# A Hymba trunk layer on one core: shorter TensorE warming, a gated and finer first load, one pair's Gram order, one row factor by square root

## The chip, the core and the metric

The kernel runs on one core of one Trainium2 chip. The metric is the device time of one execution in microseconds; lower is better. The kernel before was timed three times: 999.9, 1000.18 and 1000.47 us, median 1000.18 us.

The engines of the core have short names in the profile: PE is TensorE (matmuls), PEld its weight loads, DVE VectorE, ACT ScalarE, POOL GpSimd, SP SyncE, which here only issues transfers. L714 is line 714 of the kernel.

## The reference

One layer over 16 learned meta tokens and 512 real tokens (L = 528), width D = 2048. Cut to what matters:

```
hn = rmsnorm(h, norm_in_g)                  # 528 x 2048
P  = hn @ w_in                              # 2048 x 8320: r,k,v,g (1024 each), lora (128), B,C,h,gc (1024 each)
r,k,v,g,wl,al = shift(P[:, :4224])          # each token mixed with the one before
decay = exp(-exp(-softplus(-(w0 + tanh(wl) @ w_lora_up)) - 0.5))
a     = sigmoid(a0 + al @ a_lora_up)
kk    = normalised per head (k * k_k) ;  k = k * (1 + (a - 1) * k_a)
S_t   = S_{t-1} diag(decay_t) - (S_{t-1} kk_t)(kk_t a_t)^T + v_t k_t^T ;  y_t = S_t r_t   # 16 heads of 64
y_a   = (groupnorm(y) + bonus(r, k, v)) * silu(g)
y_b   = B * causal_conv3(C * h) * silu(gc)
h     = h + concat(y_a, y_b) @ w_out
out   = rmsnorm(h, norm_f_g)[16:]           # 512 x 2048, float32
```

## The kernel before

All large products are done in three parts to keep fp32 accuracy on a faster matmul type: each operand is split into a high part (a rounding cast, usually on ACT) and a low part (the difference, on DVE or POOL), and hi·xh, lo·xh and hi·xl are accumulated in PSUM.

**The input projection and its filler.** The normalised input is kept transposed as 16 k-tiles of 128 rows: `xh` and `xl`, made by `split_x` (L205, ACT at L207 and DVE at L208). `w_in` has 65 column tiles of 128. A load of 512 KB (`wr`, L142) brings half a tile's weights; `prefetch` and `split_w` (L132 to L144) split it into two pieces of 128x512 by an ACT cast (L134) and a DVE or POOL subtract (L135). The matmuls of one column tile run over the token ranges 0..264 and 264..528 (`FULL`), or others for tiles that leave out meta tokens, and over 16 k-tiles. The Python generator `mains()` (L483) gives all these matmuls one by one in the order of `plan`: first four column tiles (lora, k0, r0, B0) side by side, k-tile by k-tile, so that they can start as x arrives; then k, r, v, g of each head pair and C, h, B, gc. `use` reads a finished column tile.

**The order on TensorE is written out by hand.** Work that depends on other engines is issued in small steps, and between two steps `fill(ns)` (L551) takes as many matmuls from `mains()` as the given number of nanoseconds. The table `FW` (L43 to L46) holds these numbers. `until("k", i)` instead drains the generator to a named tile, so after it the order no longer depends on earlier fills. So TensorE always has matmuls of the projection to run while ACT, DVE and POOL prepare the next step.

**A head pair.** `prepare(i)` (L627, i = 0..7) computes decay and a by the low-rank products (tiles `tz`, `ta`; L571, L572, then ACT L578, POOL L639, a scan on DVE at L641 that gives `cc`), then builds the Gram matrices of nine 64-token chunks and two heads (L682) in PSUM tiles of four, four and one chunk: `za` (chunks 0 to 3), `zc` (4 to 7), `ze` (8). DVE multiplies each with a mask into `gt` (L692, six instructions). `ze` takes its two banks from the pool "main" of four banks, which the projection's column tiles (`ps_k`, `ps_r`, `ps_C` and the like) use too; `zc` takes "misc" and "ser", one bank each. After a fill come the norms (`zn`, L713, L714) and `zb` (L716), which use the banks of `zc` and `za` again. Further on, `invert` solves the triangular systems of two pairs, and `recur` (L938) runs the recurrence over the chunks; its matmuls at L957 read `ct`, which a DMA loads from the scratch `opd` in DRAM. Ahead of it stands `fill(FW["begin"])`.

**The start.** A memset of `cold` (128x512, fp32) on DVE feeds two warming matmuls into `pwarm` (L187). SP then issues four loads from `front`, an array in which the first weights and x lie in the order of use: `in_bt` (the norm gains, one weight piece of lora, x0), `in_r` (three pieces for k0, r0, B0), `in_bk` (four pieces for k-tile 1, x1) and `in_gt` (pieces for k-tiles 2 and 3, x2 and x3). Loads of weights and of x4 to x11 follow on SP. `split_piece` (L224) splits a weight piece on ACT and DVE.

**The end.** The output projection adds `mix @ w_out` to the residual; each of four blocks of 128 rows (`row` t = 0..3) gets its sum of squares (`squares`, ACT with an accumulator, L1229), and `row_scale` (L1396) makes the factor 1/sqrt: an add of the partial sums and a power -0.5 on POOL (`rsqrt`, L97). Row 1 is last: its two half blocks of 256 columns (`ends`) are added at L1453, its gain is multiplied in by `gain`, and `finish_last` scales and stores it.

Of the kernel before, what the change touches and what calls it, by code (L numbers as in the profile page):

```python
# [18 lines left out]
P = 128  # L19
DM = 2048  # L20
KT = DM // P
SEQ = 512
META = 16
L = SEQ + META
CH = 64
NCH = SEQ // CH + 1
# [18 lines left out]
    tr=3200, lev=3000, cp=4200, out=1500, begin=20300, p=2900, u=2900, s=4800, last=3700, mix=2600,  # L45
# [32 lines left out]
def hymba_kernel(ctx: ExitStack, tc: tile.TileContext, xt, xtok, front, w_in, w_out, pv, lup, cst, msk, gf, out):  # L78
# [104 lines left out]
    cold = tp.tile([P, 512], F32, tag="tm", name="cold", bufs=3)  # L183
    nc.vector.memset(cold, 0.0)
    pwarm = pi.tile([P, 512], F32, tag="ser", name="pwarm")
    for _ in range(2):
        nc.tensor.matmul(pwarm, cold[:, 0:P], cold, start=True, stop=True)  # L187
# [42 lines left out]

    for n in range(4):
        quarters[2 * n] = slot_of(2 * n)
    F0, F1, F2 = KT + P + L, 4 * P + L, 8 * P + 2 * L
    fr = [view("bt", F0), view("r0", 3 * P), view("bk", F1), view("gt0", F2)]
    o = 0
    for t in fr:
        nc.sync.dma_start(t, front[:, o : o + t.shape[1]])
        o += t.shape[1]
    ng = fr[0]
    raw[0], raw[1] = fr[0][:, KT + P : F0], fr[2][:, 4 * P : F1]  # L240
    for k in range(2):
        raw[2 + k] = fr[3][:, 8 * P + k * L : 8 * P + (k + 1) * L]
# [3 lines left out]
    nc.scalar.activation(warm, warm, AF.Tanh)  # L246
# [4 lines left out]
    with tc.manual_schedule(engines={mybir.EngineType.DVE, mybir.EngineType.Activation}):  # L251
        split_piece(0, 0, fr[0][:, KT : KT + P])
        split_x(0, slice(0, L // 2))
        split_x(0, slice(L // 2, L))
        for n in (1, 2, 3):
            split_piece(n, 0, fr[1][:, (n - 1) * P : n * P])
        split_x(1)
        for n in range(4):
            split_piece(n, P, fr[2][:, n * P : (n + 1) * P])
        for kt in (2, 3):  # L260
            split_x(kt)
            if kt == 2:
# [12 lines left out]
        head = split_x(8)  # L275
# [37 lines left out]
    HALF = SEQ // 2  # L313
# [313 lines left out]
    def prepare(i):  # L627
# [768 lines left out]
    def row_scale(t, n, eng=nc.gpsimd):  # L1396
        f = fv[:, t]
        w, v, r = f[:, 0:1], f[:, 1:2], f[:, 2:3]
        eng.tensor_scalar(out=v, in0=ssq[:, t, n : n + 1], scalar1=w, scalar2=None, op0=ALU.add)
        rsqrt(r, v)  # L1400
        scales[t] = r
# [25 lines left out]
    with tc.manual_schedule(engines={mybir.EngineType.DVE, mybir.EngineType.Activation, mybir.EngineType.Pool}):  # L1427
# [3 lines left out]
        for t in (2, 3):  # L1431
            row_part(t, 3)
            row_scale(t, 3)
        row_part(0, 3)
# [25 lines left out]
        row_scale(1, 4, nc.vector)  # L1460
        gain(1, 2, nc.vector, slice(256, 512))
        finish_last(1)


def _layout(i):
# [35 lines left out]
    front += [t[:, 1] for t in first] + [xt[:, 1]] + [t[:, 2:4].reshape(P, 256) for t in first] + [xt[:, 2], xt[:, 3]]  # L1501
# [24 lines left out]
```

## Time and profile before

| quantity | value |
|---|---|
| median of three runs | 1000.18 us |
| the profiled execution, its own time | 999.89 us |
| its span in the trace (first to last instruction) | 998.0 us |
| granted TensorE clock, mean | 0.998 |
| HBM traffic over the span | 139.28 MB read, 38.71 MB written, 178 GB/s |
| weight splits on ACT (L134) | 252 casts, 153.4 us busy |
| weight splits on POOL and DVE (L135) | 119 and 133 subtracts, 168.2 and 98.3 us busy |

The profile page gives each engine's busy time, the chain of work that ended last, and groups of instructions. In rows of the timeline the columns are the start in us from the span's start, the time in us to the end of the row's last instruction, engine, line, operation, output and inputs with shapes, how many instructions stand in the row (x4), and in brackets how long the engine had waited just before and what released it. In rows of waits the three numbers are the total in us, how often, and the longest. In the windows the columns are the stretch, its length, and the busy time of PE, PEld, DVE, ACT, POOL (with the count of instructions), the granted clock, the DMA engines' share and GB/s. Records of neighbouring matmuls overlap, since matmuls are pipelined; the distance of two starts is what one costs.

### The profile page before, as it was taken

The numbers are of one execution on the slowest core, as the hardware profiler recorded it, in microseconds if no ns is written. First come the engines' busy times: TensorE is split into PE (matmuls) and PEld (weight loads), VectorE is DVE, ScalarE is ACT, GpSimd is POOL, SyncE is SP. The second block draws the span as 40 slices with busy tenths as digits, with TensorE's granted clock in tenths as the row PEclk, the third lists the DMA queues.
The fourth block names the chain that finished last, engine by engine and source line by source line (L and its number), as shares of the span: only waits on it lengthen the run. The fifth ranks groups of instructions, "written<-read, shape, count | busy, mean of one in ns | idle before, by whom it ended". The sixth has DMA issues, their size and how long they took to land.

```text
span 998.0 us, 22792 instructions
## 1 busy us (share of the span) xinstructions
PE 986.7 (99%) x9211; PEld 910.8 (91%) x9211; DVE 689.2 (69%) x1314; ACT 412.2 (41%) x770; POOL 271.6 (27%) x286
## 2 busy tenths in 40 slices
PE   9999999999999999999999999999999999999996
PEld 8999999999998999998999998989889898888885
DVE  7777975487774579735579735246555598999895
ACT  7554432343523535232534232233332326645553
POOL 0122423133422324222324222223242423011001
PEclk9999999999999999999999999999999999999999
DMA  9527585437584365854265954978783698798634
GB/s 324 160 79 184 122 224 144 119 106 179 128 215 140 95 180 130 230 145 111 85 180 120 232 143 114 347 266 283 223 266 96 169 266 232 230 293 224 144 99 168
DMA packets 184985, 179.48 MB, mean 180 GB/s; under 512 B 112176, under 2 KB 141616, under 8 KB 184368
## 3 DMA queue, kind: packets, MB, share of 16 engines
q1 hardware_dynamic: 182288, 169.12, 58.2%
q0 software_dynamic: 2304, 8.39, 4.8%
q8 instruction: 72, 1.18, 0.5%
q10 hardware_dynamic: 288, 0.52, 0.1%
q14 instruction: 33, 0.27, 0.1%
HBM read 139.28 MB, written 38.71 MB: 178 GB/s over the span
## 4 chain that ended last, share of the span: by engine, by line
PE 95%; DMA 2%; DVE 1%; issue 1%; POOL 0%; ACT 0%; DVEq 0%; SPq 0%; POOLq 0%
PE ps_g L328 9%; PE ps_r L328 9%; PE ps_h L328 9%; PE ps_gc L328 9%; PE ps_B L328 9%; PE ps_v L328 9%; PE ps_C L328 8%; PE ps_k L328 8%; PE M L1242 8%; PE P L1242 4%; PE Q L1242 2%; PE g L682 2%; DMA ct<-opd 1%; PE ps_lora L328 1%; PE rz L957 1%; PE zs L1004 1%
## 5 line engine op out<-in xcount | busy, mean ns | idle before, releaser
L134 ACT CAST w<-wr 128x512 fp32r<-128x512 f32 x252 | 153.4, 619 | 280.0 <-PE ps_h L328 47.4
L135 POOL TENSOR_TENSOR w<-wr,w 128x512 fp32r<-128x512 f32 x119 | 168.2, 1415 | 365.2 <-ACT w L134 326.7
L135 DVE TENSOR_TENSOR w<-wr,w 128x512 fp32r<-128x512 f32 x133 | 98.3, 743 | 98.6 <-ACT w L134 97.6
L328 PE MATMUL ps_r<-xh,w 128*128 128x256 f32 (+1 forms) x512 | 95.2, 282 | 1.0 <-DVE gt L692 1.0
L328 PE MATMUL ps_k<-xh,w 128*128 128x256 f32 (+1 forms) x512 | 95.4, 284 | 0.0
L328 PE MATMUL ps_v<-xh,w 128*128 128x272 f32 (+1 forms) x512 | 95.4, 284 | 0.0
L328 PE MATMUL ps_h<-xh,w 128*128 128x258 f32 (+1 forms) x512 | 93.1, 281 | 0.0
L328 PE MATMUL ps_C<-xh,w 128*128 128x258 f32 (+1 forms) x512 | 92.5, 281 | 0.0
L328 PE MATMUL ps_g<-xh,w 128*128 128x258 f32 (+1 forms) x512 | 91.7, 280 | 0.0
L328 PE MATMUL ps_B<-xh,w 128*128 128x512 f32 x256 | 83.1, 394 | 0.0
L328 PEld LDWEIGHTS ps_r<-xh,w 128*128 128x128 f32 x512 | 80.2, 189 | 1.6 <-DVE gt L692 1.2
L328 PE MATMUL ps_gc<-xh,w 128*128 128x512 f32 x256 | 81.6, 393 | 0.0
L328 PEld LDWEIGHTS ps_k<-xh,w 128*128 128x128 f32 x512 | 80.3, 189 | 0.3
L328 PEld LDWEIGHTS ps_v<-xh,w 128*128 128x128 f32 x512 | 80.1, 189 | 0.3
L328 PEld LDWEIGHTS ps_h<-xh,w 128*128 128x128 f32 x512 | 79.5, 189 | 0.3
L328 PEld LDWEIGHTS ps_C<-xh,w 128*128 128x128 f32 x512 | 79.2, 189 | 0.6
L328 PEld LDWEIGHTS ps_g<-xh,w 128*128 128x128 f32 x512 | 79.2, 189 | 0.2
L328 PE MATMUL ps_k<-xl,w 128*128 128x256 f32 (+1 forms) x256 | 73.0, 285 | 0.0
L328 PE MATMUL ps_v<-xl,w 128*128 128x256 f32 (+1 forms) x256 | 72.5, 283 | 0.0
L328 PE MATMUL ps_h<-xl,w 128*128 128x256 f32 (+1 forms) x256 | 72.5, 283 | 0.0
L328 PE MATMUL ps_g<-xl,w 128*128 128x256 f32 (+1 forms) x256 | 72.4, 283 | 0.0
L328 PE MATMUL ps_r<-xl,w 128*128 128x256 f32 (+1 forms) x256 | 72.1, 282 | 0.0
(312 smaller groups left out, 2204.3 us busy)
## 6 DMA issues: line engine op xcount, KB each, us to landing
wr<-in_w_in_dram SPq DMA_DIRECT2D x126, 512.0 KB
ct<-opd SPq DMA_DIRECT2D x56, 320.0 KB
wo<-in_w_out_dram SPq DMA_DIRECT2D x21, 512.0 KB
opd<-gt SPq DMA_DIRECT2D x16, 576.0 KB
x<-in_w_out_dram POOLq DMA_DIRECT2D x16, 512.0 KB, 5.7
opd<-ar SPq DMA_DIRECT2D x8, 576.0 KB
opd<-bt SPq DMA_DIRECT2D x64, 64.0 KB
ct<-opd SPq DMA_DIRECT2D x16, 256.0 KB
```

The lines of the kernel that those rows point to most:

```text
L134: nc.scalar.copy(hi, rq)
L135: low[q] = eng.tensor_tensor(out=lo, in0=rq, in1=hi.bitcast(F32), op=ALU.subtract).ins
L328: nc.tensor.matmul(ps[r], ww[:, w], xx[:, kt, a:b], start=(kt == 0 and n == 0), stop=(kt == KT - 1 and n == 2))
L682: nc.tensor.matmul(z[h][:, c - c0], bk[hs, c, h : h + 2, :].rearrange("p a s -> p (a s)"), ar[hs, c].rearrange("p a s -> p (a s)"), start= ...
L957: nc.tensor.matmul(z[e][ho if e else hs, 0, k], ct[e][hs, k, o : o + CH], uv(e, k, hs, h) if part else st[hs, 4 * e + k], start=(part == 0 ...
L1004: nc.tensor.matmul(zs[hs, j], bb[:, h], uv(e, k, everything, h), start=True, stop=True)
L1242: nc.tensor.matmul(bank[s], left(prod, jj, m, s), w, start=(jj == 0 and n == 0), stop=(jj == 7 and n == 2))
```

## The change

Five places are changed.

1. `cold` and `pwarm` shrink from 512 to 128 columns, and four matmuls are issued rather than two.
2. The first loads. `in_bt`, `in_r` and `in_bk` are issued at once as before. The 1040 KB `in_gt` becomes two loads of 520 KB (weight pieces and x of k-tile 2, then those of k-tile 3), and ahead of them POOL copies one column of `in_bt` into the place that the first of them fills. So this load has to wait for the copy, and the copy for the landing of `in_bt`; all later loads stand behind it in SP's queue. The eight weight pieces of k-tiles 2 and 3 are split as 128 columns each rather than four of 256. The first weight piece's cast goes from ACT to DVE, and x0 is split at column 256 rather than 264.
3. In pair 2 alone the Gram blocks are written and masked in the order `ze`, `za`, `zc`.
4. The fill behind the Gram of pair 1 is 1700 rather than 1300 ns longer than that of the others, and the fill ahead of the recurrence is 20800 rather than 20300.
5. The factor of the last row: `row_scale(1, 4)` uses an ACT square root with the partial sum as its bias and a reciprocal on DVE rather than the DVE add and the power on POOL, and stands behind `gain`. A square root without use (its output is written over) is issued early in the end phase, behind the factors of rows 2 and 3.

```diff
-    tr=3200, lev=3000, cp=4200, out=1500, begin=20300, p=2900, u=2900, s=4800, last=3700, mix=2600,
+    tr=3200, lev=3000, cp=4200, out=1500, begin=20800, p=2900, u=2900, s=4800, last=3700, mix=2600,
...
-    cold = tp.tile([P, 512], F32, tag="tm", name="cold", bufs=3)
+    cold = tp.tile([P, P], F32, tag="tm", name="cold", bufs=3)
     nc.vector.memset(cold, 0.0)
-    pwarm = pi.tile([P, 512], F32, tag="ser", name="pwarm")
-    for _ in range(2):
-        nc.tensor.matmul(pwarm, cold[:, 0:P], cold, start=True, stop=True)
+    pwarm = pi.tile([P, P], F32, tag="ser", name="pwarm")
+    for _ in range(4):
+        nc.tensor.matmul(pwarm, cold, cold, start=True, stop=True)
...
-    F0, F1, F2 = KT + P + L, 4 * P + L, 8 * P + 2 * L
-    fr = [view("bt", F0), view("r0", 3 * P), view("bk", F1), view("gt0", F2)]
-    o = 0
-    for t in fr:
-        nc.sync.dma_start(t, front[:, o : o + t.shape[1]])
-        o += t.shape[1]
+    F0, F1 = KT + P + L, 4 * P + L
+    two = view("gt0", 2 * F1)
+    fr = [view("bt", F0), view("r0", 3 * P), view("bk", F1), two[:, 0:F1], two[:, F1 : 2 * F1]]
...
+    for n in range(3):
+        load_front(n)
     ng = fr[0]
...
+    nc.scalar.activation(warm, warm, AF.Tanh)
+    nc.gpsimd.tensor_copy(fr[3][:, 0:1], ng[:, 0:1])
+    load_front(3)
+    load_front(4)
...
-        split_piece(0, 0, fr[0][:, KT : KT + P])
-        split_x(0, slice(0, L // 2))
-        split_x(0, slice(L // 2, L))
+        nc.vector.tensor_copy(hi, w0)
+        nc.vector.tensor_tensor(out=lo, in0=w0, in1=hi.bitcast(F32), op=ALU.subtract)
+        split_x(0, slice(0, HALF))
+        split_x(0, slice(HALF, L))
...
         for kt in (2, 3):
             split_x(kt)
-            if kt == 2:
-                for n in range(4):
-                    split_piece(n, 2 * P, fr[3][:, 2 * n * P : 2 * (n + 1) * P])
+            for n in range(4):
+                split_piece(n, kt * P, fr[kt + 1][:, n * P : (n + 1) * P])
...
-        for c in range(NCH):
-            gram((za, zc, ze)[c // 4], c, c // 4 * 4)
-        for z, a, b in ((ze, 8, 9), (za, 0, 4), (zc, 4, 8)) if i == 2 else ((za, 0, 4), (zc, 4, 8), (ze, 8, 9)):
+        blocks = [(za, 0, 4), (zc, 4, 8), (ze, 8, 9)]
+        if i == 2:
+            blocks = blocks[2:] + blocks[:2]
+        for z, a, b in blocks:
+            for c in range(a, b):
+                gram(z, c, a)
+        for z, a, b in blocks:
             masked(z, a, b)
-        fill(FW["gram2"] - shift + 1300 * (i == 1) + 2000 * (i == 3))
+        fill(FW["gram2"] - shift + 1700 * (i == 1) + 2000 * (i == 3))
...
     def row_scale(t, n, eng=nc.gpsimd):
         f = fv[:, t]
         w, v, r = f[:, 0:1], f[:, 1:2], f[:, 2:3]
+        if eng is nc.scalar:
+            eng.activation(v, ssq[:, t, n : n + 1], AF.Sqrt, bias=w)
+            nc.vector.reciprocal(r, v)
+            scales[t] = r
+            return
...
             row_scale(t, 3)
+        nc.scalar.activation(fv[:, 1, 1:2], fv[:, 3, 0:1], AF.Sqrt)
         row_part(0, 3)
...
         finish(0, (3,))
-        row_scale(1, 4, nc.vector)
         gain(1, 2, nc.vector, slice(256, 512))
+        row_scale(1, 4, nc.scalar)
         finish_last(1)
```

What moves on the engines is told apart at three places. The first is the start of SP's queue, where the loads are issued (`in_g` is a weight piece, the second `in_gt` brings x4 to x7; the widths are columns of fp32). Before:

```order
L237 DMA in_bt<-in_front_dram 128x672
L237 DMA in_r_148<-in_front_dram 128x384
L237 DMA in_bk<-in_front_dram 128x1040
L237 DMA in_gt_150<-in_front_dram 128x2080
L221 DMA in_g<-in_w_in_dram 128x512
L201 DMA in_gt_157<-in_xt_dram 128x2112
```

With the change, and with what each waits for:

```order
L240 DMA in_bt<-in_front_dram 128x672
L240 DMA in_r_151<-in_front_dram 128x384
L240 DMA in_bk<-in_front_dram 128x1040
L240 DMA in_gt_149<-in_front_dram 128x1040 [waits Pool_49]
L240 DMA in_gt_149<-in_front_dram 128x1040
L221 DMA in_g<-in_w_in_dram 128x512
L201 DMA in_gt_162<-in_xt_dram 128x2112
```

The fourth load is cut in two, and its first half waits for POOL (its copy at L249); so do all loads behind it.

The second place is the Gram of pair 2 on DVE: the masks `gt` (`g_8` is `ze`, `g_0` is `za`, `g_4` is `zc`; the last number is the head). Before:

```order
L135 TENSOR_TENSOR w_2858<-wr_2856,w_2858 128x512
L692 TENSOR_TENSOR gt_2919<-g_0_0_2920,cs 128x512
L692 TENSOR_TENSOR gt_2919<-g_0_1_2921,cs 128x512
L692 TENSOR_TENSOR gt_2919<-g_4_0_2922,cs 128x512
L692 TENSOR_TENSOR gt_2919<-g_8_0_2924,cs 128x128
L692 TENSOR_TENSOR gt_2919<-g_4_1_2923,cs 128x512
L692 TENSOR_TENSOR gt_2919<-g_8_1_2925,cs 128x128
L352 TENSOR_TENSOR pr_k_2969<-ps_k_0_2801,rs 128x256
```

With the change:

```order
L135 TENSOR_TENSOR w_2870<-wr_2868,w_2870 128x512
L701 TENSOR_TENSOR gt_2935<-g_8_0_2940,cs 128x128
L701 TENSOR_TENSOR gt_2935<-g_8_1_2941,cs 128x128
L701 TENSOR_TENSOR gt_2935<-g_0_0_2936,cs 128x512
L701 TENSOR_TENSOR gt_2935<-g_0_1_2937,cs 128x512
L701 TENSOR_TENSOR gt_2935<-g_4_0_2938,cs 128x512
L701 TENSOR_TENSOR gt_2935<-g_4_1_2939,cs 128x512
L361 TENSOR_TENSOR pr_k_2981<-ps_k_0_2813,rs 128x256
```

The two small masks, which free the two "main" banks, move from the fourth and sixth place to the first two.

The third place is POOL ahead of that Gram, in the low-rank part of pair 2 (`tz` is the decay's exponent, which the scan at L641 reads). Before:

```order
L135 TENSOR_TENSOR w_2467<-wr_2462,w_2467 128x512
L358 MEMSET pr_k_2969 128x1
L639 TENSOR_SCALAR tz_2675<-tz_2675 128x576
L135 TENSOR_TENSOR w_2637<-wr_2632,w_2637 128x512
L661 COPY dd<-e_2658 128x9
```

With the change:

```order
L135 TENSOR_TENSOR w_2479<-wr_2474,w_2479 128x512
L367 MEMSET pr_k_2981 128x1
L135 TENSOR_TENSOR w_2607<-wr_2602,w_2607 128x512
L648 TENSOR_SCALAR tz_2699<-tz_2699 128x576
L670 COPY dd<-e_2674 128x9
```

A weight split now stands ahead of `tz` rather than behind it.

More of the change, by code (lines that the diff above doesn't have):

```diff
@@ L228, in split_piece, with load_front @@
         nc.vector.tensor_tensor(out=lo[:, cols], in0=t, in1=hi[:, cols].bitcast(F32), op=ALU.subtract)
+    HALF = SEQ // 2
     for n in range(4):
         quarters[2 * n] = slot_of(2 * n)
[L233 to L242 removed]
+    F0, F1 = KT + P + L, 4 * P + L
+    two = view("gt0", 2 * F1)
+    fr = [view("bt", F0), view("r0", 3 * P), view("bk", F1), two[:, 0:F1], two[:, F1 : 2 * F1]]
+    def load_front(n):
+        o = sum(t.shape[1] for t in fr[:n])
+        nc.sync.dma_start(fr[n], front[:, o : o + fr[n].shape[1]])
+    for n in range(3):
+        load_front(n)
+    ng = fr[0]
+    raw[0] = fr[0][:, KT + P : F0]
+    for k in range(1, 4):
+        raw[k] = fr[k + 1][:, 4 * P : F1]
+    nc.scalar.activation(warm, warm, AF.Tanh)
+    nc.gpsimd.tensor_copy(fr[3][:, 0:1], ng[:, 0:1])
+    load_front(3)
+    load_front(4)
     later_w = [load_w(0, "g")]
@@ L245, in hymba_kernel @@
     later_w += [load_w(1, "xT1"), load_w(2, "e1"), load_w(3, "xT0")]
-    nc.scalar.activation(warm, warm, AF.Tanh)
     load_x("ar", 8, 2)
@@ L1500, in _layout @@
     front = [pv[:, V_NG : V_NG + KT], first[0][:, 0], xt[:, 0]] + [t[:, 0] for t in first[1:]]
-    front += [t[:, 1] for t in first] + [xt[:, 1]] + [t[:, 2:4].reshape(P, 256) for t in first] + [xt[:, 2], xt[:, 3]]
+    for k in range(1, 4):
+        front += [t[:, k] for t in first] + [xt[:, k]]
     front = np.concatenate(front, 1)
```

3 lines of the change are left out of this document (2 added, 1 removed).

## The prediction

> **What bounds the kernel now.** I read the page first: busy times, the clock row, the chain of work that ended last.
>
> ```profile
> PE 986.7 (99%) x9211; PEld 910.8 (91%) x9211; DVE 689.2 (69%) x1314; ACT 412.2 (41%) x770; POOL 271.6 (27%) x286
> PEclk9999999999999999999999999999999999999999
> PE 95%; DMA 2%; DVE 1%; issue 1%; POOL 0%; ACT 0%; DVEq 0%; SPq 0%; POOLq 0%
> ```
>
> TensorE is busy for 986.7 of 998.0 us and makes up 95% of the chain. The change leaves no matmul of the layer out, so it can only win the few places where TensorE stands still, slow down the start, or make new gaps. The waits of PE name the gaps:
>
> ```profile
> PE pwarm L187 <- DVE cold L184: 1.4, 1, 1.4
> PE ps_r L328 <- DVE gt L692: 1.0, 1, 1.0
> PE rz L957 <- DMA ct<-opd: 0.3, 1, 0.3
> ```
>
> Each stands for one event. The change touches the place of all three, a stall at x1 that the timeline of the start shows, and the tail behind the last matmul. The profiled execution took 999.89 us, 0.29 under the median of the three; its span is 998.0, so 1.89 us lie outside. The sum below is made against 999.89.
>
> **The start: warming and first loads.** The timeline of the first 10 us, rows of PE, ACT and DVE picked out:
>
> ```profile
> 1.45 3.75 PE L187 MATMUL pwarm<-cold 128*128 128x512 f32 x4 [1.45 <-DVE cold L184]
> 3.86 0.30 ACT L227 CAST w<-in_bt 128x128 fp32r<-128x128 f32 x1 [1.63 <-DMA in_bt<-in_front_dram]
> 4.06 0.92 ACT L207 ACTIVATE xh<-in_bt 128x264 fp32r<-128x264 f32 x2
> 5.28 0.41 PE L495 MATMUL ps_lora<-xh,w 128*128 128x256 f32 x2
> 7.12 0.74 ACT L207 ACTIVATE xh<-in_bk,in_bt 128x528 fp32r<-128x528 f32 x1 [1.55 <-DMA in_bk<-in_front_dram]
> 7.89 0.77 DVE L208 SCALAR_TENSOR_TENSOR xl<-in_bk,in_bt,xh 128x528 fp32r<-128x528 f32 x1 [1.77 <-ACT xh L207]
> 7.68 0.40 PE L328 MATMUL ps_B<-xh,w 128*128 128x512 f32 x1
> 8.10 0.38 PE L328 MATMUL ps_lora<-xh,w 128*128 128x256 f32 x1
> 8.71 0.39 PE L328 MATMUL ps_lora<-xl,w 128*128 128x256 f32 x1 [0.23 <-DVE xl L208]
> ```
>
> The four warming records (two matmuls) last from 1.45 to about 5.1, 0.94 us each, so warming holds TensorE until then, though x0's first half is ready by about 4.06 + 0.46 = 4.52. Between the rows at 5.28 and 7.68 sixteen matmuls of some 256 columns and two of 512 start: 0.12 and 0.24 us each. The first k-tile has 18 and three of them, 2.88 us, and ends at 7.68 + 0.24 = 7.92; in effect it begins at 5.04. The next one's first matmul comes at 8.10 and its second, due at 8.22, at 8.71: 0.18 + 0.49 = 0.67 us lost, because `xl` of x1 ends at 8.66, its cast having waited for `in_bk` until 7.12.
>
> After: four matmuls of 128 columns are half the work of two of 512: about 1.45 + 3.75 / 2 = 3.3 by these rows, ahead of the landing at 3.86. The landing becomes the start. The x casts no longer stand behind the weight cast on ACT (4.06-3.86 = 0.20 earlier): first half at about 4.32, second at 4.8, with `xl` following on DVE. I put the effective start at 4.8, where the second half is there too: **-0.25 us**. For x1 the landing decides. What the three loads left at once hold is 336 + 192 + 520 = 1048 KB (widths 672, 384 and 1040 in the listed rows, times 512 bytes). The windows of the start give what DMA moved (last column):
>
> ```profile
> 1.00:2.00 1.00, 0.55 (x1) 0.50 (x2) 0.39 (x1) 1.00 (x1) 1.00 (x6) 1.00 0.30 35
> 2.00:3.00 1.00, 1.00 (x2) 0.34 (x1) 0.00 (x0) 0.22 (x2) 0.26 (x2) 1.00 0.82 253
> 3.00:4.00 1.00, 1.00 (x2) 0.34 (x1) 0.00 (x0) 0.14 (x1) 0.00 (x0) 1.00 1.06 378
> 4.00:5.00 1.00, 1.00 (x3) 0.29 (x1) 0.68 (x2) 1.00 (x4) 0.00 (x0) 1.00 0.94 383
> ```
>
> 35 + 253 + 378 + 383 = 1049 KB by 5.0. With no later load sharing the queues, `in_bk` lands at about 5.3 rather than 7.1 (bounds 5.0 and 7.1). Then `xh` is ready by 6.1 and `xl` by 6.9, before TensorE ends the first k-tile at 4.8 + 2.88 = 7.68, and the **0.67 us** go.
>
> The price is the gate. What stands behind it on SP is every later load. Before, `in_gt` was issued at 2.12; now POOL's copy waits for the landing at 3.86 and the issue comes at about 4.2.
>
> ```profile
> 2.12 0.43 SPq L237 DMA_DIRECT2D in_gt<-in_front_dram  x1
> 14.24 2.81 DVE L208 SCALAR_TENSOR_TENSOR xl<-in_gt,in_bt,xh 128x528 fp32r<-128x528 f32 x4 [0.41 <-ACT xh L207]
> 17.40 0.28 PE L328 MATMUL ps_lora<-xh,w 128*128 128x256 f32 x1
> ```
>
> The bytes are the same, so only idle DMA time is lost: between 0 (none idle) and 2.1 us (the whole difference). A load issued at 0.73 shows bytes only in the window from 2.0 on, so 4.2 becomes some 5.4, and the first three loads keep DMA busy until 5.1 or so: I take 0.4 us. The cover is x4 to x7: the last `xl` ends at 17.05; the matmuls on these four k-tiles begin at 17.40, and the first that reads this `xl` is some ten later, at 18.6: 1.5 us of cover. The earlier start uses 0.9 and the delay 0.4, together 1.3. So no stall at my value; at the upper bound 0.9 + 2.1 - 1.5 = 1.5 us show. Splitting the pieces of k-tiles 2 and 3 finer adds four casts on ACT and four subtracts on DVE, each with little more than the row's fixed part; they lie in the same cover. Start in all: **-0.9**, bounds -0.9 and +0.6.
>
> What the rows cannot show is whether the clock comes up. In the first 5 us the matmuls are slow (the first at full pace is at 5.28, 3.8 us after the warming began), although the PEclk row reads 9. After the change TensorE is idle from about 3.3 to 4.4. By the Trainium skill, "TensorE: Matmul & The Clock Gate", section Part 1: The HAM clock gate, the clock is halved by default and full only after about 3.4 us of sustained work, in a free-running window. By that rule this warming is too short, which is the first rival below; the trace agrees in that 3.8 us passed.
>
> **Pair 1.** The norms at L713 and L714 come 0.13 apart; `zb` had to wait for the bank `ser`, which the last `gt` mask gives free:
>
> ```profile
> 130.21 0.29 PE L714 MATMUL n_tz<-sq_l,ones 128*2 128x288 f32 x1
> 130.63 0.47 PE L716 MATMUL zb<-rk_h,ones 128*128 128x512 f32 x1
> ```
>
> 0.42 - 0.13 = 0.29 us. The fill that is 400 ns longer puts four more matmuls of 0.12 ahead, 0.48: the wait goes, **-0.3** (bounds -0.3 and 0).
>
> **Pair 2.** `ps_r` needs the two "main" banks of `ze`, but its masks stood fourth and sixth of
>
> ```profile
> 217.99 2.87 DVE L692 TENSOR_TENSOR gt<-g,cs 128x512 f32<-128x512 f32 x6
> 220.11 0.38 PE L328 MATMUL ps_r<-xh,w 128*128 128x256 f32 x1 [0.96 <-DVE gt L692]
> ```
>
> With both small masks first they are done some 0.5 us after the Gram is, and `ps_r`, due at 219.0 to 219.1, finds banks. Against that, the order on POOL puts a weight split ahead of `tz`:
>
> ```profile
> 199.07 1.67 POOL L639 TENSOR_SCALAR tz<-tz 128x576 f32<-128x576 f32 x1 [3.21 <-ACT tz L578]
> 200.70 1.30 POOL L135 TENSOR_TENSOR w<-wr,w 128x512 fp32r<-128x512 f32 x1
> 200.78 2.43 DVE L641 TENSOR_TENSOR_SCAN cc<-smask,tz 128x576 f32<-128x576 f32 x1 [3.81 <-POOL tz L639]
> 239.45 1.36 DVE L641 TENSOR_TENSOR_SCAN cc<-smask,tz 128x576 f32<-128x576 f32 x1 [0.23 <-POOL tz L639]
> ```
>
> `tz` ends about 1.9 later (ACT's cast first, then 1.30, from 199.6), at 202.6. But the scan took 2.43 beside POOL's split and 1.36 in pair 3 without; it would now run beside none and end at 203.96 rather than 203.21: the chain is 0.75 late. Its masks first leave room for that: the Gram's last `ze` mask is ready near 219.0, just when needed. Taken **-0.95**; bounds -1.1 (all of it) and 0 (the chain is later still).
>
> **Recurrence start.** `rz` waits 0.33 for `ct`. Four more matmuls of the projection ahead (500 ns) cover it, and the load's issue doesn't move: **-0.4** with the small gaps of the next `rz`, bounds -0.5 and 0.
>
> **The tail.** The factor of the last row is on the path, no matmul is left:
>
> ```profile
> 990.98 0.19 ACT L1229 ACTIVATION_READ_ACCUMULATOR sqj<-xb 128x1 f32 x1
> 991.20 0.21 DVE L1399 TENSOR_SCALAR fv<-ssq,fv 128x1 f32<-128x1 f32 x1
> 991.33 0.41 DVE L1300 TENSOR_TENSOR xb<-xb,gfb 128x256 f32<-128x256 f32 x1
> 991.49 0.66 POOL L98 TENSOR_TENSOR fv<-fv,mhalf 128x1 f32<-128x1 f32 x1 [4.33 <-DVE fv L1399]
> 992.19 0.48 DVE L1418 TENSOR_SCALAR xb<-xb,fv 128x512 f32<-128x512 f32 x1 [0.44 <-POOL fv L98]
> 2.03 0.20 ACT L246 ACTIVATE warm<-warm 128x1 f32<-128x1 f32 x1
> 233.47 0.25 DVE L757 RECIPROCAL nd<-nd 72x16 f32<-72x16 f32 x1
> ```
>
> Now the sum, the add and the power run 991.17 to 992.19, 1.0 us. After: the square root on ACT at 0.20 (nearest small ACT row) beside `gain` on DVE (991.2 to 991.55), then the reciprocal at 0.25: the outputs start at about 991.8, **-0.4**. The square root needs another table; the load of one took 1.28 at the start. It is issued with the early dummy, where ACT waits:
>
> ```profile
> 0.73 1.28 ACT L246 ACT_TABLE_LOAD   x1 [0.73 <-PEq L1513]
> 979.01 0.63 ACT L1229 ACTIVATE sqj_None<-xb 128x512 f32<-128x512 f32 x1 [1.07 <-DVE xb L1223]
> 987.78 0.42 ACT L1229 ACTIVATE sqj<-xb 128x256 f32<-128x256 f32 x1 [0.84 <-DVE xb L1453]
> ```
>
> 1.07 there and 0.84 later are more than it takes; without the cover up to 1.28 would show: bounds -0.4 and +0.9.
>
> **The sum.** -0.9 - 0.3 - 0.95 - 0.4 - 0.4 = -2.95. TensorE's order shifts by four matmuls from pair 1 to 3 and again from the recurrence on, and this schedule had such a wait at each of the places above; I allow one new one of the size of `rz`'s, +0.35. -2.6 in all: 999.89 - 2.6 = **997.3 us**.
>
> **Rivals.** *The clock stays low* (slower window). If 3.6 us or so of unbroken work are needed, counted from the new block at 4.8, the clock rises at about 8.4. Matmuls until then take twice their time, so 3.6 us do the work of 1.8: the start loses 1.8 against my forecast, +0.9 rather than -0.9. The sum is 997.3 + 1.8 = 999.1. For it: the slow rows until 5.0. Against: the warming still runs for about 1.8 us, and a monitor might count that. By the same page's free-running window the rise lies between 7.8 and 11.2, a sum between 998.8 and 1000.5.
>
> *The gate shows.* If the idle DMA time is the whole 2.1, 1.5 us of stall appear before k-tiles 4 to 7: 998.8. Against: DMA is busy until 5.1 in the windows.
>
> *Pair 2 only moves.* The chain through POOL and DVE is late by more than 0.75, `ar` and `bk` come later than the fill, and the wait stands at the Gram or stays at `ps_r`: 998.3 with the wait as large as before, 999.3 with one more us.
>
> *Slower.* The clock stays halved past the first window, because TensorE waits in between for k-tiles 2 and 3 and the count begins anew. Each us of half clock costs 0.5, so the whole gain of 2.6 is eaten by a rise at 4.8 + 2 x 2.6 = 10.0; from there on it is slower than before, and from 14.0 on by 2 us, 1001.9. For it: TensorE is idle just before 4.8 and x2 and x3 come later than they did. Against: at half pace TensorE needs its operands later (x1 at 10.6 rather than 7.7), so it waits less, and then works unbroken.
>
> **How the numbers follow.** My forecast has 0.60, the low clock 0.16, the gate 0.07, pair 2 0.08, the slower side 0.09. The forecast alone is good for 996.1 to 998.2 (all gains at their bounds; one or two small waits more). The range takes in the low clock and the gate: 995.9 to 999.5. Below 0.2%, 2.0 us, a change of this kernel can't be told from none, so faster means under 998.2: nearly all of the forecast and some of the pair 2 case, 0.62. Within it lie most of the low clock, the gate and the rest of pair 2: 0.28. Slower: 0.10, the slower side and the far end of the low clock.
>
> **What would show it.** Right: the warming ends before 3.9, full pace (0.12 apart) from the first `ps_lora` on; `in_bk` lands near 5.3; no wait before `xl` of x1 and of x4 to x7; `zb` 0.13 behind the norms; no wait of `ps_r` on `gt`; `rz` without a DMA wait; one table load behind row 3's factor, the last scale at 400 ns behind the last accumulator rather than 1.0. Wrong: matmuls 0.24 apart until 8 us or later, a wait for x2 to x7, a wait on `gt` or on `ar` and `bk` near 219.

## The result and the profile after

| kernel | runs | median us | lowest to highest |
|---|---|---|---|
| before | 18 | 1000.20 | 998.80 to 1001.37 |
| changed | 18 | 998.59 | 997.48 to 1000.36 |

The ratio of changed to before is 0.9985, 95% interval 0.9979 to 0.9992: about 1.5 us (0.8 to 2.1) less. The profiled executions are 999.89 before and 998.63 after, 1.26 less. Single executions far above the rest (1075 us of the kernel before, 1624 and 1914 us in two of the experiments, at a granted clock of 0.56 to 0.94) are left out of all ratios and means. The forecast was 997.3 within 995.9 to 999.5. The range holds the result, but the gain is little more than half of the 2.6 that was forecast: the change does less than its parts promised.

The page of the changed kernel, rows as shown of before:

```profile
span 996.8 us, 22815 instructions
PE 986.1 (99%) x9215; PEld 912.9 (92%) x9215; DVE 687.3 (69%) x1319; ACT 413.8 (42%) x776; POOL 268.4 (27%) x286
PEclk9999999999999999999999999999999999999999
PE 98%; DVE 1%; DMA 0%; ACT 0%; issue 0%; DVEq 0%; ACTq 0%
```

The chain has lost its DMA part, and TensorE is 98% of it rather than 95%. The waits of PE:

```profile
PE ps_lora L504 <- DVE w L263: 1.1, 1, 1.1
PE pwarm L187 <- DVE cold L184: 1.0, 1, 1.0
PE tz L580 <- DVE xT L932: 0.3, 1, 0.3
PE prs L489 <- DVE rs L487: 0.2, 1, 0.2
```

The waits of `ps_r` for `gt` and of `rz` for `ct` are gone. New is a wait ahead of the first k-tile, behind the shorter warming, and a wait of `tz` for a copy on DVE. Why some 2 us of waits taken away give so little is seen in the first 10 us (start, time, engine, line, operation, count):

```profile
1.05 2.08 PE L187 MATMUL pwarm<-cold 128*128 128x128 f32 x8 [1.05 <-DVE cold L184]
4.25 1.45 PE L504 MATMUL ps_lora<-xh,w 128*128 128x256 f32 x4 [1.13 <-DVE w L263]
7.26 0.41 PE L337 MATMUL ps_r<-xh,w 128*128 128x256 f32 x1
7.47 0.41 PE L337 MATMUL ps_r<-xl,w 128*128 128x256 f32 x1
9.40 0.59 PE L337 MATMUL ps_B<-xh,w 128*128 128x512 f32 x1
9.82 0.28 PE L337 MATMUL ps_lora<-xh,w 128*128 128x256 f32 x1
9.95 0.28 PE L337 MATMUL ps_lora<-xl,w 128*128 128x256 f32 x1
```

Two matmuls of 256 columns start 0.21 apart at 7.3 and 0.12 to 0.13 apart from 9.8 on. TensorE runs its whole first k-tile at half pace, until 9.8, where before the change it was at full pace from about 5.0. The trace's own record of the granted clock says the same: it begins with the rise to full clock, at 9.81 here and at 5.04 before. So `in_bk` came earlier, as intended, to a TensorE that needed x1 only at 9.8.

The account at four places of the program, in us of TensorE's time, after against before (starts of the same matmul in both traces; up to pair 3 the order of TensorE differs by some matmuls, so the places are taken where it doesn't):

| place | before | after | shift | gained since |
|---|---|---|---|---|
| first `prs` (L477, L486 after) | 49.99 | 50.97 | +1.0 | -1.0 |
| Gram of pair 4 | 352.42 | 352.01 | -0.4 | 1.4 |
| first M of the output projection | 861.80 | 860.42 | -1.4 | 1.0 |
| end of the span | 998.0 | 996.8 | -1.2 | -0.2 |

### The profile page after: what moved, and what is told of

Its sections match the earlier page's. It is cut to its first block, busy times and chain, and to the rows that moved or that the text cites. A ratio compares the mean times of both kernels' runs of the same rounds, so it can differ in the third digit from the quotient of the medians.

```text
span 996.8 us, 22815 instructions
## 1 busy us (share of the span) xinstructions
PE 986.1 (99%) x9215; PEld 912.9 (92%) x9215; DVE 687.3 (69%) x1319; ACT 413.8 (42%) x776; POOL 268.4 (27%) x286
## 4 chain that ended last, share of the span: by engine, by line
PE 98%; DVE 1%; DMA 0%; ACT 0%; issue 0%; DVEq 0%; ACTq 0%
PE ps_k L337 9%; PE ps_r L337 9%; PE ps_h L337 9%; PE ps_C L337 9%; PE ps_g L337 9%; PE ps_gc L337 9%; PE ps_B L337 9%; PE ps_v L337 9%; PE M L1255 8%; PE P L1255 4%; PE Q L1255 2%; PE g L691 2%; PE ps_lora L337 1%; PE rz L970 1%; PE zs L1017 1%; PE zy L1021 1%
## 5 line engine op out<-in xcount | busy, mean ns | idle before, releaser
L337 PE MATMUL ps_C<-xl,w 128*128 128x256 f32 (+1 forms) x256 | 71.9, 281 | 0.0
```

The source lines that it names most:

```text
L337: nc.tensor.matmul(ps[r], ww[:, w], xx[:, kt, a:b], start=(kt == 0 and n == 0), stop=(kt == KT - 1 and n == 2))
```

## The experiments

Twelve kernels were run, each with its own runs beside the kernel before on the same chip, 10 or 11 of each. All are the changed kernel with the edit shown.

**The changed kernel a second time** (no edit).

> The changed kernel as it is, profiled a second time. In its first profile the matmuls keep half pace until 9.6 us, 5.4 us after the first block begins at 4.25. Theory W (the clock rises at the end of the first stretch of a free-running clock window, about 3.4 us long, in which TensorE was busy throughout): the rise lies anywhere between 4.25 + 3.4 = 7.7 and 4.25 + 6.8 = 11.1 and differs from one execution to the next. Theory C (a count of unbroken work that starts with the block): the rise is at 9.6 again, within 0.2. Time by both 998.6, single runs 997.5 to 1000.4.

998.84 (ratio 0.9986, 0.9978 to 0.9995). The clock is up at 9.2 this time, which fits theory W and not theory C with its 9.6 within 0.2 (9.8 before that).

The clock records of the traces show more than the two times. In all 14 profiles of this case, the rise and the fall of the clock behind the last matmul lie a whole number of times 3.413 us apart: 288, 289 or 290 times (983.04, 986.45 or 989.87 us). So the clock changes on a grid of 3.413 us, whose place against the kernel's start differs from profile to profile. And in all 14 the rise stands at the end of the first stretch of this grid in which TensorE was busy throughout (but for 0.05 us in one of them). In the changed kernel's first profile the stretches that end at 2.99 and at 6.40 hold idle time, before the warming and behind it (3.13 to 4.25); the one that ends at 9.81 holds none. This is theory W.

**Seven warming matmuls.**

```diff
-    for _ in range(4):
+    for _ in range(7):
         nc.tensor.matmul(pwarm, cold, cold, start=True, stop=True)
```

> Seven warming matmuls rather than four, so that warming ends at about 1.05 + 7 x 0.47 = 4.35 and TensorE has no idle stretch before the first k-tile at 4.25; nothing else differs. Theory W: the rise lies between 4.5 and 7.9, on average 3.2 us earlier than in the changed kernel, worth 1.6 us; of that up to 0.9 may come back as a wait for x4 to x7, whose last xl ended at 18.5 with a need at 19.6 in the changed kernel's profile. 997.0 to 997.9 against 998.6. Theory C: the rise is at 1.05 + 5.4 = 6.4, 997.0 to 997.5. Rival S (the slow first matmuls have nothing to do with warming, but with the transfers that land beside them): the rise stays at 9.6 and the time at 998.6.

```profile
1.05 3.36 PE L187 MATMUL pwarm<-cold 128*128 128x128 f32 x14 [1.05 <-DVE cold L184]
4.30 1.07 PE L504 MATMUL ps_lora<-xh,w 128*128 128x256 f32 x4
5.49 0.28 PE L337 MATMUL ps_k<-xh,w 128*128 128x256 f32 x1
7.60 0.29 PE L337 MATMUL ps_lora<-xh,w 128*128 128x256 f32 x1
8.12 0.39 PE L337 MATMUL ps_lora<-xl,w 128*128 128x256 f32 x1 [0.23 <-DVE xl L208]
```

These rows are the same stretch. Full pace comes at 4.8, within theory W's bounds and not at theory C's 6.4, and x1's first matmul at 7.60 rather than 9.82. Rival S, that warming doesn't matter, is out. 0.4 us of waiting for `xl` of x1 shows again, now that TensorE is early enough for it, and no wait for x4 to x7. The time is 998.28 (0.9980, 0.9972 to 0.9989): 0.6 less than the changed kernel on the same chip, and not the 0.7 to 1.6 expected.

**Seven matmuls without the gate.** The same, and POOL's copy left out:

```diff
-    nc.gpsimd.tensor_copy(fr[3][:, 0:1], ng[:, 0:1])
```

> Seven warming matmuls, and POOL's copy ahead of the fourth load left out, so that all loads are issued at once; the two smaller transfers stay. If the gate does what it should, in_bk lands later than with it (7.1 as before the change rather than about 6.4) and x1 makes TensorE wait 0.3 to 0.7 where the clock is already up; x4 to x7 are there 0.5 to 1.5 earlier. Against the run with seven matmuls and the gate: 0 to +0.5 if x1 decides, -0.3 to -0.9 if x4 to x7 decide.

998.38 (0.9982, 0.9973 to 0.9991). In the trace the clock is up at 4.4, but x1's first two matmuls come at 8.24 and 8.86 rather than 7.60 and 8.12, 0.64 and 0.74 later, and 0.73 is still there at the Gram of pair 1. (In all four profiles with the gate and unbroken warming x1's second matmul comes at 8.01 to 8.12.) The gate is worth 0.7 us of TensorE's time once the clock is up; in the time 0.1 of it is seen, which the noise covers.

**The gate alone taken away** (four matmuls).

> The changed kernel with its four warming matmuls and without POOL's copy: the gate alone taken away. Theory: while the clock is low TensorE needs x1 only at about 9.8, so neither the earlier x1 nor the later x4 to x7 is on its path and the time stays at 998.6 within 0.3. Rival: the gate delays x2 to x7 so much that it costs, and the time falls by 0.5 or more.

998.56 (0.9987, 0.9978 to 0.9996), and x1's first matmul at 9.88 against 9.82. With the clock low the gate gives nothing and costs nothing: theory held.

**The same short warming, later.**

```diff
-    cold = tp.tile([P, P], F32, tag="tm", name="cold", bufs=3)
-    nc.vector.memset(cold, 0.0)
+    cold = tp.tile([P, 512], F32, tag="tm", name="cold", bufs=3)
+    for _ in range(3):
+        nc.vector.memset(cold, 0.0)
...
-        nc.tensor.matmul(pwarm, cold, cold, start=True, stop=True)
+        nc.tensor.matmul(pwarm, cold[:, 0:P], cold[:, 0:P], start=True, stop=True)
```

> The changed kernel with the same four warming matmuls, but two more memsets and wider ones ahead of them on DVE, so that they run from about 2.3 to 4.4 and end where the first k-tile begins: as much warming as in the change, without the idle stretch behind it. Theory W (the clock looks at stretches of some 3.4 us that don't follow the kernel's own events, and rises at the end of one in which TensorE was busy throughout): the rise lies between 2.3 + 3.4 = 5.7 and 9.1. Theory U (3.65 to 3.85 us of unbroken work, as in the kernel before and with seven warming matmuls): the rise is at 6.0 to 6.2. Theory F (stretches at a fixed place from the kernel's start, one ending near 5 and one between 9.2 and 10): 9.2 to 10, as in the change. Time: 998.6 less half of what the rise comes earlier, so 997.0 to 997.3 by U, 998.6 by F.

Warming ran from 2.76 to 4.84 without an idle stretch behind it, and the clock was up at 8.3: within theory W's bounds (2.76 + 3.4 to 2.76 + 6.8), later than theory U's 2.76 + 3.85 = 6.6 and earlier than theory F's 9.2. The time is 997.99 (0.9984, 0.9975 to 0.9993), which the noise doesn't tell apart from the changed kernel (0.9985). So to leave no idle stretch is not enough when the warming begins late.

**No warming at all.** (The four matmuls, `cold` and `pwarm` are left out.)

> The changed kernel without any warming matmul and without the memset for it. Theory W: the rise lies between 4.25 + 3.4 = 7.7 and 11.1, so the change's short warming is worth nothing: 998.6 as the changed kernel. Theory U: 4.25 + 3.8 = 8.1, earlier than in the change (9.2 to 9.9), 998.0. Theory F: 9.2 to 10. Rival (the short warming helps in part): the rise later than 10 and the time 999 or more.

Full pace at 10.5, within theory W's bounds and not at theory U's 8.1; 998.78 (0.9988, 0.9979 to 0.9997). The change's four matmuls, with an idle stretch behind them, do no measurably more than none.

**The old warming put back alone.**

```diff
-    cold = tp.tile([P, P], F32, tag="tm", name="cold", bufs=3)
+    cold = tp.tile([P, 512], F32, tag="tm", name="cold", bufs=3)
...
-    pwarm = pi.tile([P, P], F32, tag="ser", name="pwarm")
-    for _ in range(4):
-        nc.tensor.matmul(pwarm, cold, cold, start=True, stop=True)
+    pwarm = pi.tile([P, 512], F32, tag="ser", name="pwarm")
+    for _ in range(2):
+        nc.tensor.matmul(pwarm, cold[:, 0:P], cold, start=True, stop=True)
```

> The changed kernel with the old warming alone put back: two matmuls of 128x512 (a few rows of DVE and ACT near 20 us stand in another order by it). Theory: without an idle stretch behind warming the clock is up by about 5.1, as before the change; the first k-tile begins in effect at 5.0 to 5.1, x1 is there (no wait, since in_bk lands at 6.4), so the matmuls at 50 us come 1.3 to 1.7 earlier than in the changed kernel. If nothing gives this back the time is 997.0 to 997.4; seven short matmuls gave 0.7 at the end of 1.6 at the start, so I expect 997.6 to 998.0. Rival S (warming doesn't decide): 998.6.

```profile
1.45 3.74 PE L187 MATMUL pwarm<-cold 128*128 128x512 f32 x4 [1.45 <-DVE cold L184]
7.67 0.40 PE L337 MATMUL ps_B<-xh,w 128*128 128x512 f32 x1
7.90 0.28 PE L337 MATMUL ps_lora<-xh,w 128*128 128x256 f32 x1
8.02 0.28 PE L337 MATMUL ps_lora<-xl,w 128*128 128x256 f32 x1
```

The same stretch again: x1 follows x0 without a gap, which is what the other half of the change (gate, smaller loads) was for. The cast of x1 starts at 5.58 here; in all eleven profiles with the gate it starts at 5.55 to 6.60, in the three without it at 7.12 to 7.27. The profiled execution took 996.67, 1.96 less than that of the changed kernel, with the last matmul 1.96 earlier as well, but it is the fastest of the ten; the median is 997.94 (0.9979, 0.9970 to 0.9989). Over the three kernels with unbroken warming and the gate (this one, seven matmuls, and seven with row 0's stores moved, below) the mean of 31 runs is 997.94, over 29 of the changed kernel 998.65: 0.71 less, with a 95% interval of about 0.33 either way (0.60 less when each run is taken against the kernel before on its own chip).

**Pair 2 as before.**

```diff
-        if i == 2:
-            blocks = blocks[2:] + blocks[:2]
...
-        for z, a, b in blocks:
+        for z, a, b in (blocks[2:] + blocks[:2] if i == 2 else blocks):
             masked(z, a, b)
```

> The changed kernel with the Gram blocks of pair 2 written and masked as before the change (the masks of ze fourth and sixth on DVE); nothing else moves. Theory: ps_r waits for the masks again, for 0.9 to 1.5, and all of it is left at the last matmul: 999.5 to 1000.1. Rival (the wait is only taken from one further on): the last matmul moves by less than 0.4, 998.6 to 999.0.

```profile
PE ps_r L337 <- DVE gt L701: 0.7, 1, 0.7
```

This row of PE's waits is back; the matmul comes 0.87 later than its usual distance, and the Gram of pair 4 comes at 353.10 rather than 352.01, of which 0.2 stand already at pair 1. The time is 999.80 (0.9996, 0.9988 to 1.0005), 1.2 more than the changed kernel. Pair 2 is most of what the change gains at the end, and theory, not rival, held.

**The old factor of the last row.**

```diff
-        nc.scalar.activation(fv[:, 1, 1:2], fv[:, 3, 0:1], AF.Sqrt)
...
+        row_scale(1, 4, nc.vector)
         gain(1, 2, nc.vector, slice(256, 512))
-        row_scale(1, 4, nc.scalar)
```

> The changed kernel with the old factor of the last row (DVE add, POOL power, ahead of gain) and without the early square root. Theory D (after the last matmul the output transfers set the end: DMA is busy without a gap from 988.8 to 994.5 and the four last stores only queue up): the last scale starts 0.45 later, but the end moves by less than 0.2: time 998.6 within 0.3. Rival E (the factor is on the path): +0.45, 999.0. The trace tells them apart by the time from the last matmul's start to the end of the span, 8.35 in the changed kernel, 8.17 before.

998.35 (0.9985, 0.9976 to 0.9994): no slower. The last scale starts 2.36 behind the start of the last matmul rather than 1.91, as expected, and the span ends 8.21 behind it rather than 8.35. So the square root does what it should on its own path and is worth nothing at the end. Theory E is out. Theory D's words for it, though, had to be tried:

**Row 0 stored earlier.**

```diff
         gain(1, 3, nc.vector)
+        finish(0, (2, 0))
...
                 gain(1, 2, nc.vector, cols)
-                finish(0, (2, 0))
```

> The changed kernel with the scaling and storing of row 0's columns 0 to 1023 and 1024 to 1535 (768 KB) moved ahead of the last two half blocks in the order of DVE, ACT and SP; before it stood behind the first half block. Theory D (behind the last matmul the stores alone set the end, DMA without a gap for 5.7 us at 385 GB/s): the stores of row 0 go into the half idle stretch 984 to 989, and the time behind the last matmul falls from 8.35 by 0.4 to 1.0: 997.6 to 998.2. Rival E (the last row's chain sets the end, or its stores' own latency): no change, 998.6.

998.81 (0.9988, 0.9979 to 0.9996), 8.28 behind the last matmul: no gain. Theory D is out too in the form in which it was put: taking 768 KB from the queue behind the last matmul doesn't let the end come earlier.

**Seven matmuls and row 0 stored earlier.**

> Seven warming matmuls together with the earlier stores of row 0. If the gain of warming is lost behind the last matmul, where the stores queue up (9.06 and 8.86 there in two kernels with seven matmuls), it comes back here: 997.0 to 997.4. If it is lost before, in the sums of DVE and the loads of w_out that they wait for (2.4 us of such waits in the changed kernel, 5.4 with seven matmuls): 997.7 to 998.1.

997.95 (0.9977, 0.9968 to 0.9987), with full pace from 5.4. The last matmul came 1.4 earlier than in the changed kernel, but the end of the span 9.19 behind it. The earlier scaling of row 0 stands ahead of the last half blocks on DVE, and makes DVE late for them: the last scale starts 2.72 behind the start of the last matmul rather than 1.91, and these 0.8 us are what the end loses. So this run doesn't tell whether the gain of seven matmuls alone is lost in the stores.

**Seven matmuls and four gains on POOL.**

```diff
-        at((34, 35, 38, 39, 41, 42, 44, 46)[n], gain, n // 2, n % 2, nc.vector)
+        at((34, 35, 38, 39, 41, 42, 44, 46)[n], gain, n // 2, n % 2, nc.gpsimd if n > 3 else nc.vector)
```

> Seven warming matmuls, and the last four of the eight multiplications of xa by its gain (128x512, 0.69 each on DVE) moved to POOL, which is idle for most of that stretch. With seven warming matmuls the last matmul came 1.0 to 1.3 earlier than in the changed kernel but the time from it to the end grew from 8.35 to 9.06. Theory V (DVE is full from 845 to 975, its sums for rows 2 and 3 run behind TensorE and start the outputs late): 2.8 us less on DVE brings the time behind the last matmul back to 8.4, and the time to 997.3 to 997.7 against 998.3. Rival D (the stores alone set the end) or POOL slowing DVE beside it: still 9.0, 998.3.

1001.13 (1.0009, 1.0000 to 1.0018), slower than with seven matmuls alone by 2.8. The profiled execution, 999.26, is one of the faster of its runs and shows 1.3 of the 2.8. What the theory left out stands in the rows of DVE beside POOL's gains:

```profile
915.35 1.28 DVE L1228 TENSOR_TENSOR o<-x,o 128x512 fp32r<-128x512 f32 x2
918.13 1.46 POOL L1313 TENSOR_TENSOR xa<-xa,gfb 128x512 f32<-128x512 f32 x1 [0.21 <-ACT sqj_None L1242]
918.35 0.68 DVE L1236 TENSOR_TENSOR xa<-xa,P 128x512 f32<-128x512 f32 x1
920.66 2.67 DVE L1228 TENSOR_TENSOR o<-x,o 128x512 fp32r<-128x512 f32 x2
921.17 1.61 POOL L1313 TENSOR_TENSOR xa<-xa,gfb 128x512 f32<-128x512 f32 x1
932.24 0.89 POOL L1214 DMA_DIRECT2D x<-in_w_out_dram  x1 [9.46 <-DVE o L1228]
```

Two instructions of DVE at L1228 took 1.28 with POOL idle and 2.67 beside a gain on POOL. In all, four DVE instructions beside the four gains took 1.19 to 2.07 rather than 0.69 each, 4.1 us more, while only 4 x 0.69 = 2.8 us of work were taken off DVE. (The one at 918.35, which reads a PSUM tile, was not slowed.) So POOL slowing DVE, the last of the rivals, is what happened, at a higher price than it was given; between 911 and 932 us TensorE falls about 0.5 further behind. POOL also issues the transfers that add blocks of `w_out` into `x`. The one at 932.24 goes out 2.3 later than with seven matmuls alone, but POOL had waited 9.46 us for DVE by then, so the gains didn't hold it up. The run neither proves nor refutes that DVE's sums are late by too much work.

The best of these is the changed kernel with the old warming (997.94), level with seven matmuls and the earlier stores of row 0 (997.95) and with the later short warming (997.99).

## Why the prediction was right or wrong

The range 995.9 to 999.5 holds the result because it was drawn to take in the first rival; the interval of the forecast alone, 996.1 to 998.2, misses it. That the time is no further off is in part luck: the start was 1.9 worse than forecast and the tail 0.6, and 1.1 more than forecast was gained between them.

**The start: wrong, and the first rival right.** The forecast had -0.9 here and the trace shows +1.0. The step that failed is "The landing becomes the start": the sum let the first block run at full pace, as if warming were done when its matmuls are (3.3), and the low clock stood only in a rival with a chance of 0.16. What the runs showed in its place is that the clock rises at the end of a stretch of 3.413 us without idle time; the 1.1 us of idle behind the shorter warming broke that stretch, and the first k-tile ran at half pace until 9.8. The rival "the clock stays low" put the rise at 8.4 and the cost at 1.8; the rise came at 9.2 to 9.8 in the changed kernel's two profiles and the shift against the forecast was 1.9. Its time, 999.1, is 0.5 above the median because the middle of the program gained 1.1 more than forecast, and the tail 0.6 less. Shown by runs: unbroken warming from 1.05 or 1.45 on brings the clock up at 4.4 to 5.4 (six kernels, the one before among them), short warming with a gap at 8.0 to 10.4 (six profiles), short warming without a gap from 2.76 on at 8.3, none at 10.5. Putting the old warming back alone gives a median of 997.94, 0.6 above the forecast, and 996.67 in the fastest of its runs, the profiled one.

The Trainium skill, "TensorE: Matmul & The Clock Gate", section Part 1: The HAM clock gate, says that the clock follows a free-running window of about 3.4 us and that one busy window is needed. An estimate from this figure puts the rise 3.4 to 6.8 us behind the start of unbroken work. The profiles agree: 3.6 to 6.2 us in the seven where this work begins at 4.2 to 4.5, 5.5 with the later warming, and 3.4 to 4.3 in the six where it begins at 1.05 or 1.45. These six all lie in the first 1.0 of 3.4 us; whether that is chance, or something ties the grid to the start of the kernel, stays open.

**The loads: right, but not where it counted.** `in_bk` was there for a cast at 6.43 rather than 7.12 (I had 5.3; the earliest profile with the gate has 5.55). The fourth load was issued at 3.99, and x4 to x7 were never waited for, even with the clock up: the last `xl` of these four ends at 16.5 with the old warming, 17.1 with seven matmuls and 18.5 in the changed kernel, against 17.05 before, so the gate's delay is lost in what the landings differ by from run to run.

**Pairs 1 and 2: right.** -0.3 and -0.95 were forecast, less 0.35 for one new wait: -0.9. The trace shows -1.4 between the first `prs` and pair 4. The masks as they ran:

```profile
203.24 1.36 DVE L650 TENSOR_TENSOR_SCAN cc<-smask,tz 128x576 f32<-128x576 f32 x1 [5.44 <-POOL tz L648]
218.56 2.86 DVE L701 TENSOR_TENSOR gt<-g,cs 128x128 f32<-128x128 f32 x6
219.78 0.28 PE L337 MATMUL ps_r<-xh,w 128*128 128x256 f32 x1
```

The scan took 1.36 beside no work on POOL, as assumed, and the two small masks freed the banks ahead of `ps_r`, which came without a wait. The allowance was the right size too: the wait of `tz` (0.3 in the list, 0.4 over its usual distance) is it. Not foreseen was that the wait at L870 (0.38 in the trace before) goes. Pair 2's part is shown by the run that puts it back; what pair 1 and the recurrence gained is read from the two traces alone.

**Recurrence start: mis-sized.** -0.4 was taken for the first `rz` group; this group of 32 matmuls gave 0.78 (1.40 to 0.62 from its first start to the start behind it), and the matmuls around it 0.2: -1.0 from pair 4 to the output projection. The wait that the list named stood among three smaller ones in the same group.

**The tail: wrong.** -0.4 was forecast and the span's end is 0.2 later behind the last matmul (8.2 to 8.4 in the eight profiles with the new factor and without seven matmuls, 8.2 in the two with the old factor). The rows of the factor are as reckoned, and the table load for the square root stands where ACT has time, as planned (it waits 1.1 and 3.2 us for others further on):

```profile
975.65 1.28 ACT L1452 ACT_TABLE_LOAD   x1
989.82 0.29 ACT L1413 ACTIVATE fv<-ssq,fv 128x1 f32<-128x1 f32 x1
989.82 0.43 DVE L1313 TENSOR_TENSOR xb<-xb,gfb 128x256 f32<-128x256 f32 x1
990.16 0.16 DVE L1414 RECIPROCAL fv<-fv 128x1 f32<-128x1 f32 x1
990.36 0.48 DVE L1436 TENSOR_SCALAR xb<-xb,fv 128x512 f32<-128x512 f32 x1
```

The step that failed is to end the path at "the outputs start": behind it stand the stores. Windows of before (last columns: clock, DMA share, GB/s):

```profile
993.00:993.50 0.50, 0.00 (x0) 0.00 (x0) 0.50 (x1) 0.00 (x0) 0.24 (x1) 1.00 0.00 0
995.50:996.00 0.50, 0.00 (x0) 0.00 (x0) 0.00 (x0) 0.00 (x0) 0.00 (x0) 0.50 1.02 377
996.00:996.50 0.50, 0.00 (x0) 0.00 (x0) 0.00 (x0) 0.00 (x0) 0.00 (x0) 0.50 0.68 238
```

and of after:

```profile
992.50:993.00 0.50, 0.00 (x0) 0.00 (x0) 0.00 (x0) 0.00 (x0) 0.00 (x0) 0.85 1.04 389
994.00:994.50 0.50, 0.00 (x0) 0.00 (x0) 0.00 (x0) 0.00 (x0) 0.00 (x0) 0.50 0.97 356
994.50:995.00 0.50, 0.00 (x0) 0.00 (x0) 0.00 (x0) 0.00 (x0) 0.00 (x0) 0.50 0.09 33
```

Before, DMA stood idle for half a us at 993 waiting for the last row, and then ended at full rate. After, it hardly waits there (225 GB/s from 991.5 to 992.0), but the last bytes come at a rate of 33 GB/s, a small part of what the engines do, until nearly 995. The last packet lands 6.56 behind the start of the last matmul, against 6.64 before: of 0.45 won on the factor 0.1 reach the landing. From there to the end of the span it is 1.8 rather than 1.6. The run with row 0's stores moved has the same 6.57 although DMA stood idle before the last four stores. Why the last packets trail in the kernels with the square root, and not with the old factor, stays open.

**What a gain at the start is worth at the end.** With unbroken warming the first `prs` comes 1.3 to 1.9 us earlier than in the changed kernel's two profiles, the time falls by 0.7. In two of the three profiles (seven matmuls with and without the earlier stores) the end of the span moves from 8.35 to 9.1 behind the last matmul. DVE's rows of the last half block, with seven matmuls and in the changed kernel:

```profile
987.71 0.42 DVE L1472 TENSOR_TENSOR xb<-xb,end 128x256 f32<-128x256 f32 x1
```

```profile
988.77 0.42 DVE L1472 TENSOR_TENSOR xb<-xb,end 128x256 f32<-128x256 f32 x1 [0.66 <-PE end L1468]
```

In the first DVE comes straight from other work to a product that has been there for 0.3 us; in the second it has waited for TensorE. So there DVE's chain is late. With seven matmuls alone this is 0.24 of the 0.7 (the last scale starts 2.15 behind the last matmul rather than 1.91). The rest lies behind it, in the stores: two that are issued 0.5 and 0.04 ahead of the last matmul in the changed kernel go out 0.5 and 1.0 behind it, and the four last stores queue up behind these; the last packet lands 7.40 behind the last matmul rather than 6.56. With row 0 stored earlier all of it is in DVE's chain, as said above. What makes DVE late may stand in its waits between 780 and 985 us, first with seven matmuls, then in the changed kernel:

```profile
DVE wo L1218 <- DMA wo<-in_w_out_dram: 5.4, 3, 2.4
```

```profile
DVE wo L1218 <- DMA wo<-in_w_out_dram: 2.4, 3, 1.1
```

5.4 and 5.7 us of waits for loads of `w_out` in the two that lose the gain, 3.9 in the old warming's, which keeps it. But three kernels with a late TensorE have as much (5.6 with the old factor, 5.5 without the gate, 6.4 with row 0 stored earlier) and lose nothing. So that the loads of the output projection set a pace of their own, which an earlier TensorE runs into, is a guess that these waits don't settle and no experiment shows; moving work to POOL was the wrong test. A rival is untested too: all three profiles happen to have the rise early (4.8 to 5.4), while the grid allows 4.5 to 8.3 for warming from 1.05 or 1.45 on. So the runs without a profile may simply gain less at the start than these three.

## What to carry to other kernels

Warming has to begin early and run on, without an idle stretch, into the first real matmul. What counts is when this unbroken work begins, not the number of warming matmuls: in all 14 profiles full pace came 3.4 to 6.2 us behind that beginning. Look at the distance of the first matmuls rather than at the clock row. A step that is shortened ahead of transfers is worth only what the last landing moves. And a gain of TensorE early in a long kernel has to be followed to the end, since a later stage with loads of its own may give it back.

## What the runs showed of the hardware

The granted clock reads 1.00 in every window of the first 10 us, while matmuls of 256 columns start 0.21 apart until 9.8 and 0.12 apart then: the row doesn't show the low clock ahead of its first rise, since the clock record has no entry there. At the end it does, falling to 0.5 some 4.1 us behind the last matmul (the window 992.5 to 993.0 has 0.85, so the fall is near 992.85, and the last matmul ends near 988.75). Over the 14 profiles the fall comes 2.1 to 4.8 us behind the last matmul's end, on the same grid of 3.413 us as the rise. The stretches of the grid that end with the fall held up to 1.3 us of matmuls, while those that held 2.0 us or more didn't end with it; ahead of the rise, stretches with up to 2.8 us of matmuls didn't bring the clock up.

A DVE instruction that combines two 128x512 tiles and takes 0.69 us with POOL idle took 1.19 to 2.07 beside a multiplication of the same size on POOL; one that read one of its tiles from PSUM took 0.68 beside it.
